# A two-layer hybrid decoder trunk: another opening, with positions and rotary tables taken early, one sum of squares, and more low parts made by DMA

## The chip, the cores and the metric

The kernel runs on one core of one Trainium2 chip. The metric is the device time of one execution in microseconds, as the median of several. The profile is one further execution with its instructions recorded; its times are counted from the span's start.

## The reference

The model has two layers over 512 tokens of width 1024. Layer 0 mixes tokens by retention (four heads, rotary positions on q and k), layer 1 by an mLSTM; each is followed by a convolutional feed-forward block of width 2816, and everything is normalised, shifted, scaled and gated by columns computed from a conditioning row c. Cut to what this change touches:

```python
c_act = silu(c)
for i in range(2):
    mod = c_act @ ada_w[i] + ada_b[i]
    sh_t, sc_t, gt_t, sh_f, sc_f, gt_f = split(mod, 6)
    h = rmsnorm(x, norm_tok_g[i]) * (1 + sc_t) + sh_t
    y = retention(h, positions, ...) if i == 0 else mlstm(h, ...)
    x = x + gt_t * y
    h = rmsnorm(x, norm_ffn_g[i]) * (1 + sc_f) + sh_f
    x = x + gt_f * conv_ffn(h, ...)
return rmsnorm(x, final_g)
# in retention:
proj = h @ w_in                     # q, k, v, g
ang = positions[..., None] * inv_freq
q, k = rope(q, cos(ang), sin(ang)), rope(k, cos(ang), sin(ang))
```

All is float32. The matrix products reach that precision with a split: a value is a high part in TensorE's single-pass float32 form plus a low part (the value less its high part), and a product is high by high, high by low and low by high.

## The kernel before, in words

Activations lie with features on the partitions: eight tiles x[0] to x[7] of 128 features by 512 tokens. Weights come in 128x1024 chunks. ScalarE casts a chunk to its high part (`high_part`), VectorE subtracts for the low part (`low_part`). The other way to a low part, `low_part_added`, has ScalarE write minus the high part and GpSimd issue an accumulating DMA that adds the raw chunk onto it.

**The planner.** Nothing is issued directly. Each call to an engine is recorded with the buffers that it reads and writes (`Plan.add`). A call gets an estimated cost: for TensorE by output width, with a factor for plain float32 operands; for DMAs by size. In `Plan.order` TensorE's costs are summed in program order, and a call of another engine is due 30 us after the TensorE time at which it was written, or earlier if a successor's due time, a cost and a latency ask for it. `Plan.run` then simulates the engines: each takes, among calls whose inputs are ready, the one with the earliest due time, and does not begin one that would hold up an urgent one. A call that opens a new buffer may not start over 30 us (`EARLY`) ahead of its due time. Calls made while `plan.pin` is set keep their written order on each engine. `after` adds an order to another call without data between them. The order that comes out is the order of the instructions on each engine; SP's DMA issues are planned in the same way.

**The opening** is `ret_start`. Loads of x, of c's row (`c_row`), an identity, columns of parameters (`vecs`), rows of the conditioning weights (`ada`) and weight chunks (`raw`, from `w_s0`) go through SP's queue. TensorE spreads c over the partitions (`pc`, plain float32 with one row), ScalarE puts it through silu into `c_ext`, and each modulation column is then one VectorE instruction over 1025 elements (`gemv`), the conditioning weights times `c_ext` with a running sum. Beside that ScalarE squares seven tiles of x and VectorE the eighth; VectorE adds them in three groups, whose sums TensorE contracts in three groups of one-column matmuls (`means`, tile `pms`). The root and reciprocal of the four columns are spread over partitions and tokens: VectorE writes four diagonal blocks (`diag`), and TensorE multiplies them by ones. `scaled` multiplies x by gain and root (`xr`), ScalarE adds the shift and casts (`hh`), VectorE makes the low part (`hl`). `busy(n)` puts dummy matmuls of 512 columns on TensorE: 3, 5, 2, 3 and 8 of them, in this order.

Then a loop over the eight tiles (`products`) multiplies h by the weights of head 0's v and g into eight PSUM banks, 24 matmuls a tile (`pst`, `pc`). Each step needs, from VectorE, two `gemv`, a gain, `scaled`, a weight's low part and h's low part.

After the loop come, in program order, the load of the positions (`posi`), the centering of v, the gate's silu, and `rope_tables`: a chain of 32 VectorE instructions over 128x512 (an argument reduction in `ra`, `rk`, `rn`, `rr`), then sine and cosine by ScalarE and GpSimd. Head 0's q and k follow as four chunks of 24 matmuls (`pp`), then `rope`, and for the later heads products folded in the manner of Strassen, whose operands (`t24`, `t3` and a rewritten half of h) VectorE makes in `sums_early`. The folded products (`p`) of head 1's q and k come next on TensorE.

**The end** is `End`, the last norm. The final contraction runs over the first 256 tokens of all eight tiles, then over the second 256. During the second half `later` is called after each tile: it makes the first half's root, and then calls `use_early`, which does nothing here; all output scalings and stores of the first half are written in `rest`, after the last contraction.

Of the kernel before, what the change touches and what calls it, by code (L numbers as in the profile page):

```python
# [16 lines left out]
P = 128  # L17
# [29 lines left out]

KINDS = {"s": NSLOTS, "w": WTILES, "a": 2, "ps": 8, "vm": 4, "dsh": 4}
HURRY = 1.5
SHARE = 1.4  # L50
EARLY = 30.0

# [4 lines left out]
VEC = {}  # L57
_at = 0
for _n, _w in (
    ("ntok", 2 * KT), ("nffn", 2 * KT), ("final", KT), ("rgn", 16), ("mgn", 16),  # L60
    ("mcw", 4 * 16), ("mcb", 16), ("fcw", 2 * 3 * 44), ("fcb", 2 * 44), ("bg", 2), ("inv", 1),
):
    VEC[_n] = _at
    _at += _w
# [72 lines left out]

class Call:
    __slots__ = ("eng", "name", "obj", "a", "k", "bufs", "preds", "succs", "occ", "lat", "dma", "due", "left", "ready",
                 "new", "fn", "pin", "after", "end", "shared")  # L140


class Plan:
    LAT = dict(PE=0.23, DVE=0.18, ACT=0.18, POOL=0.2, SP=0.1)

    def __init__(self):
        self.calls, self.pin = [], None

    def engine(self, eng, obj):
        plan = self  # L150
# [7 lines left out]
    def add(self, eng, obj, name, a, k):  # L158
        c = Call()
        c.eng, c.obj, c.name, c.a, c.k = eng, obj, name, a, k  # L160
        c.preds, c.succs, c.fn, c.pin, c.after = set(), [], None, self.pin, None
        n = len(self.calls)
        views = [(v, m == 0) for m, v in enumerate(a) if isinstance(v, View)]
        views += [(v, key == "accum_out") for key, v in k.items() if isinstance(v, View)]
        c.bufs = list({id(v.buf): v.buf for v, _ in views}.values())
        for v, w in views:
            self.note(n, c, v, w)
        c.dma = 0.0
        width = max([v.width for v, _ in views])
        if name == "dma_start":  # L170
            size = max((v.box[1] - v.box[0]) * v.width for v, _ in views) * 4e-6
            c.dma = size * (5.4 if "accum_op" in k else 2.45) + 0.05
            c.occ = 0.9 if eng == "POOL" else 0.4
        elif eng == "PE":
            o = a[0].width
            single = a[2].buf.args[2] == F32R and not any(s[0] == "bitcast" for s in a[2].steps)
            c.occ = max(o * 4.427e-4, 0.06) * (1 if single else 4)
        elif eng == "DVE":
            if name == "reciprocal":
                c.occ = 0.05 + 6.45e-3 * width  # L180
            elif name in ("tensor_scalar", "tensor_copy", "memset"):
                c.occ = 0.12 + 4.5e-4 * width
            else:
                c.occ = 0.09 + 1.06e-3 * width + (0.1 if "accum_out" in k else 0)
        elif eng == "ACT":
# [26 lines left out]
    def order(self):  # L212
# [26 lines left out]
            c.left = len(c.preds)  # L239

        for c in calls:
            c.due = pe_time + (0.0 if c.eng == "PE" else 30.0)
            pe_time += c.occ * (c.eng == "PE")
        for n in range(len(calls) - 1, -1, -1):
            c = calls[n]
# [12 lines left out]
    def run(self):  # L258
# [20 lines left out]
        def start_of(n, at):  # L279


            c = calls[n]
            t, need = max(at, c.ready), {}
            for b in c.bufs:
                if b.bufs and b.log is not None:
                    need[b.key] = need.get(b.key, 0) + 1
                    if bisect(makers[b.key], b.maker) > len(room[b.key]):
                        return None
            for key, k in need.items():
                if len(room[key]) < k:  # L290
# [89 lines left out]
def trunk(ctx: ExitStack, tc: tile.TileContext, xT, cb, pos, vec, ident, decay, zmask, ada, w_s0, w_in0, w_v0,  # L380
# [58 lines left out]
    posi = slot("posi", I32)  # L439

    def col(name, i):
        return vecs[:, VEC[name] + i : VEC[name] + i + 1]
# [749 lines left out]
    class End(Norm):  # L1192
# [348 lines left out]
    def ret_start():  # L1541
# [25 lines left out]
            wh[k] = high_part(raw[k])  # L1567

        def low(k):
            wl[k] = low_part(raw[k], wh[k])  # L1570

        def square(m):
            sq[m] = slot("sq")
            if m < 7:
# [4 lines left out]
        def add(a, b):  # L1579
            V.tensor_tensor(sq[b][:], sq[a][:], sq[b][:], op=ALU.add)  # L1580

        def means(m, last):

            for t in range(4):
                PE.matmul(ps[:, t : t + 1], sq[m][:, t * P : t * P + P], ones["d"][:, :1].bitcast(F32),
                          start=(m, t) == (3, 0), stop=last, skip_group_check=True)

        def products(k):
            hi, lo, st, sp = wh[k], wl[k], k == 0, k == KT - 1
# [7 lines left out]
        plan.pin = uid("pin")  # L1597
# [6 lines left out]
        S.dma_start(vecs[:, : VEC["nffn"]], vec[:, : VEC["nffn"]])  # L1604
        load_ada(KT)
        load_ada(0)
        load_raw(0)
# [5 lines left out]
        S.dma_start(vecs[:, VEC["nffn"] :], vec[:, VEC["nffn"] :])  # L1613
        silu_c = lambda i: A.activation(c_ext[:, i * T : i * T + T], pcs[i][:], AF.Silu)
        square(0)
        square(1)
        add(0, 1)
        silu_c(0)
        square(2)
        add(1, 2)  # L1620
        silu_c(1)
        square(3)
        add(2, 3)
        square(4)
        square(5)
        square(7)
        add(4, 5)
        square(6)
        add(6, 7)
        A.activation(rc[:, :1], eps_t[:], AF.Sqrt)  # L1630
        busy(5)
        means(3, False)
        busy(2)
        means(5, False)
        means(7, True)
# [3 lines left out]
        diag = slot("diag")  # L1639
        busy(3)  # L1640
        for t in range(4):
            cs = slice(t * P, t * P + P)
            V.tensor_scalar(diag[:, cs], eye[:, :P], rc[:, t : t + 1], None, op0=ALU.mult)
        for t in range(2):
            cs = slice(*HALVES[t])
            PE.matmul(ps[:, cs], ones["1"][:].bitcast(F32), diag[:, cs], start=True, stop=True,
                      skip_group_check=True)
        gain(0, 0, 0)
        gemv(0, 0, mod[0])
        high(0)  # L1650
        busy(8)
# [12 lines left out]
        for k in range(KT):  # L1664
            if k + 1 < KT:
                if k + 2 < KT:
# [7 lines left out]
                gemv(0, k + 1, mod[k + 1])  # L1674
# [3 lines left out]
        S.dma_start(posi[:], pos.broadcast_to([P, T]))  # L1678
# [4 lines left out]
        for _ in rope_tables():  # L1683
            pass
        return xrs

    def nothing(j):
# [11 lines left out]
    def ret_q(i, between=nothing):  # L1699
# [36 lines left out]
    def gates(ps):  # L1736
# [31 lines left out]
        S.dma_start(zm[:], zmask)  # L1768

    def conv_then(i, name, kt):  # L1770
        ch = (0 if name == "q" else 8) + i * 2 + kt
# [236 lines left out]
```

## Time and profile before

| | us |
|---|---|
| median of 3 runs | 1502.32 |
| lowest, highest run | 1498.59, 1504.9 |
| the profiled execution | 1497.61 |
| its span, first to last instruction | 1495.8 |
| TensorE busy in the span | 1468.1 |
| VectorE busy | 1264.9 |
| ScalarE busy | 1069.4 |
| GpSimd busy | 285.3 |

Nearly all instructions carry the same line number (that of the call in `Plan.issue`), so rows are told apart by tile names: output, an arrow, inputs, with buffer numbers left out. PE is TensorE's matmuls, PEld its weight loads, DVE VectorE, ACT ScalarE, POOL GpSimd, SP the sync engine. A row of the timeline has start, duration, engine, operation, tiles, shapes, a count, and in brackets how long the engine was idle before it and what ended that. Plain float32 products show as two rows for one matmul. Granted clock is the share of TensorE's clock that was allowed.

### The profile page before, as it was taken

To read this page: it belongs to the slowest core of one execution; us is meant where nothing else is said; L and a number is where in the kernel's file an instruction comes from. 1 tells how busy PE (TensorE), PEld (TensorE's weight loads), DVE (VectorE), ACT (ScalarE), POOL (GpSimd) and SP (SyncE) were. 2 spreads that over 40 slices of the span, in tenths; PEclk is the share of its full clock that TensorE was granted. 3 is DMA by queue.
4 is the path that set the end of the run, shared out by engine and by line. 5 is a ranking of instruction groups with operands and counts; after the bars stand their busy time and mean duration, and the time that the engine had idled before them with its cause. 6 is when DMAs were issued, how large, how long until landed. Compare 5 with 4: busy or idle time off the path is not lost.

```text
span 1495.8 us, 27226 instructions
## 1 busy us (share of the span) xinstructions
PE 1468.1 (98%) x10477; PEld 1373.1 (92%) x10477; DVE 1264.9 (85%) x2141; ACT 1069.4 (71%) x1601; POOL 285.3 (19%) x311
## 2 busy tenths in 40 slices
PE   9989999999999999999999999999999999999997
PEld 6889999998999999989999998999889899999997
DVE  6999979678988989888897999888889887877786
ACT  4558768877587766666569985889856876767652
POOL 0234223322111111111001231223231111111100
PEclk9999999999999999999999999999999999999998
DMA  9567989997788999999367995899796988877741
GB/s 376 162 162 178 293 193 242 226 284 203 180 225 213 251 246 265 254 243 267 110 195 155 238 230 148 184 230 211 234 261 176 220 224 197 206 191 168 196 130 57
DMA packets 92980, 315.00 MB, mean 211 GB/s; under 512 B 12193, under 2 KB 14625, under 8 KB 92850
## 3 DMA queue, kind: packets, MB, share of 16 engines
q0 software_dynamic: 31824, 115.88, 41.9%
q1 hardware_dynamic: 61026, 197.38, 37.8%
q8 instruction: 82, 1.34, 0.3%
q14 instruction: 48, 0.39, 0.1%
HBM read 195.23 MB, written 2.12 MB: 132 GB/s over the span
## 4 chain that ended last, share of the span: by engine, by line
PE 81%; DMA 7%; DVE 6%; issue 2%; ACT 2%; POOL 1%; DVEq 0%; POOLq 0%; SPq 0%; ACTq 0%
PE p L376 34%; PE po L376 23%; PE pv L376 7%; PE pp L376 5%; PE pf L376 4%; PE pav L376 3%; DMA wb<-w_up 2%; PE psc L376 2%; PE pst L376 2%; DMA wlo<-ws 2%; DMA ada<-ada 1%; DVE ada L376 1%; ACT whi L376 1%; DVE wlo L376 1%; DVE ws L376 1%
## 5 line engine op out<-in xcount | busy, mean ns | idle before, releaser
L376 PE MATMUL p<-hl,whi 128*128 128x256 f32 x992 | 275.5, 278 | 0.7 <-DVE hl L376 0.5
L376 PE MATMUL p<-hh,whi 128*128 128x256 f32 (+1 forms) x994 | 275.6, 278 | 0.0
L376 PE MATMUL p<-hh,wlo 128*128 128x256 f32 x992 | 273.9, 278 | 0.0
L376 ACT ACTIVATE wlo<-whi 128x1024 fp32r<-128x1024 f32 x221 | 233.2, 1060 | 54.9 <-PE po L376 25.3
L376 PEld LDWEIGHTS p<-hl,whi 128*128 128x128 f32 x992 | 187.1, 189 | 1.4 <-DVE hl L376 1.1
L376 PEld LDWEIGHTS p<-hh,whi 128*128 128x128 f32 x994 | 187.5, 189 | 0.4
L376 PEld LDWEIGHTS p<-hh,wlo 128*128 128x128 f32 x992 | 186.3, 188 | 0.1
L376 PE MATMUL p<-t24h,whi 128*128 128x256 f32 x744 | 166.7, 281 | 7.6 <-ACT fs L376 5.5
L376 PE MATMUL po<-ggl,whi 128*128 128x512 f32 (+1 forms) x448 | 153.2, 343 | 0.0
L376 PE MATMUL po<-ggh,wlo 128*128 128x512 f32 (+1 forms) x448 | 152.7, 343 | 0.0
L376 PE MATMUL po<-ggh,whi 128*128 128x512 f32 (+1 forms) x448 | 152.3, 343 | 0.0
L376 DVE SCALAR_TENSOR_TENSOR x<-po,mod,x 128x512 f32<-128x512 f32 (+1 forms) x184 | 112.6, 627 | 32.7 <-PE po L376 32.3
L376 PE MATMUL p<-t24l,whi 128*128 128x256 f32 x496 | 138.0, 278 | 0.0
L376 PEld LDWEIGHTS p<-t24h,whi 128*128 128x128 f32 x744 | 127.1, 189 | 11.4 <-ACT fs L376 6.9
L376 ACT CAST whi<-raw 128x1024 fp32r<-128x1024 f32 (+1 forms) x117 | 117.5, 1017 | 25.9 <-PE pf L376 4.6
L376 POOL DMA_DIRECT2D wlo<-wa x62 | 54.4, 878 | 411.4 <-ACT wlo L376 303.8
L376 DVE SCALAR_TENSOR_TENSOR ada<-ada,c_ext 128x1025 f32<-128x1025 f32 x96 | 120.1, 1252 | 7.0 <-DMA ada<-ada 7.0
L376 PE MATMUL po<-yh,whi 128*128 128x256 f32 (+1 forms) x354 | 116.0, 329 | 0.2 <-DVE x L376 0.2
L376 PE MATMUL po<-yl,whi 128*128 128x256 f32 (+1 forms) x352 | 115.9, 329 | 0.0
L376 PE MATMUL po<-yh,wlo 128*128 128x256 f32 (+1 forms) x352 | 115.2, 329 | 0.0
L376 DVE SCALAR_TENSOR_TENSOR cv<-p,vecs,cv 128x511 f32<-128x511 f32 (+1 forms) x144 | 106.2, 743 | 7.5 <-ACT cv L376 7.2
L376 ACT CAST whi<-ws 128x1024 fp32r<-128x1024 f32 x86 | 90.1, 1050 | 29.0 <-DVE ws L376 19.6
(285 smaller groups left out, 4428.3 us busy)
## 6 DMA issues: line engine op xcount, KB each, us to landing
ada<-ada SPq DMA_DIRECT2D x96, 512.5 KB, 7.2
wlo<-ws POOLq DMA_DIRECT2D x73, 512.0 KB, 7.4
wlo<-wa POOLq DMA_DIRECT2D x62, 512.0 KB, 6.9
wlo<-wt POOLq DMA_DIRECT2D x44, 512.0 KB, 6.9
wlo<-raw POOLq DMA_DIRECT2D x36, 512.0 KB, 8.4
wa<-w_up SPq DMA_DIRECT2D x36, 512.0 KB, 6.7
wb<-w_up SPq DMA_DIRECT2D x36, 512.0 KB, 6.8
raw<-w_o SPq DMA_DIRECT2D x32, 512.0 KB, 8.1
```

Source lines behind the costliest of these rows:

```text
L376: getattr(c.obj, c.name)(*[real(v) for v in c.a], **{key: real(v) for key, v in c.k.items()})
```

## The change

- **Loads.** c's row is the first load, x comes right behind it. The positions and the first columns of `vecs` are issued by ScalarE instead of SP. `inv` moves to the front of `vecs`, so that it comes with these columns. The weight chunk of tile 0 is loaded ahead of the second row of conditioning weights, and the remaining columns and the mask `zm` later.
- **Planner.** A call can carry `soon`, its offset from TensorE's time in place of the 30 us; it then also has no `EARLY` limit. Plain float32 matmuls are priced 8 instead of 4 times the single-pass ones, and the least price is 0.05 instead of 0.06.
- **Tables.** `rope_tables` is recorded at the beginning of `ret_start`, unpinned, with an offset of 200.
- **Squares.** ScalarE squares all tiles but x[3]; VectorE squares that and adds all eight in one chain; one group of `means` is left. The Sqrt dummy moves behind the square of x[4].
- **Roots.** No diagonals: each column of the reciprocal, repeated 128 times, is the weights of one product with the identity.
- **Dummies.** 3, 9, 1 and 1 instead of 3, 5, 2, 3 and 8.
- **Low parts.** Tiles 5, 6 and 7 of the loop, and the second chunks of head 0's q and k, use `low_part_added`.
- **End.** `use_early` scales and stores the first half's tiles during the second half, four at a time.

The diff, cut to its core:

```diff
+ROPE_DUE = 200.0
+BUSY = (9, 1, 1)
+LOWK = 5
+QLOW = (1, 3)
...
-            c.occ = max(o * 4.427e-4, 0.06) * (1 if single else 4)
+            c.occ = max(o * 4.427e-4, 0.05) * (1 if single else 8)
...
-            c.due = pe_time + (0.0 if c.eng == "PE" else 30.0)
+            c.due = pe_time + (0.0 if c.eng == "PE" else 30.0 if c.soon is None else c.soon)
...
-                t = max(t, c.due + lag - EARLY)
+                if c.soon is None:
+                    t = max(t, c.due + lag - EARLY)
...
+    c_load = len(plan.calls)
+    plan.soon = -8.0
     S.dma_start(c_row[:1, :D], cb)
     for m in range(KT):
-        S.dma_start(x[m][:], xT[m])
+        S.dma_start(x[m][:], xT[m]).after = c_load
+    plan.soon = -15.0
+    A.dma_start(vecs[:, : VEC["nffn"]], vec[:, : VEC["nffn"]])
+    A.dma_start(posi[:], pos.broadcast_to([P, T]))
+    plan.soon = None
...
         def use_early(self, k):
-            pass
+            if k in (2, 4):
+                self.use(0, 2 * k - 4, 2 * k)
         def rest(self):
-            item([], lambda w: self.use(0, 0, 4))
-            item([], lambda w: self.use(0, 4, 8))
...
-            wl[k] = low_part(raw[k], wh[k])
+            wl[k] = (low_part if k < LOWK else low_part_added)(raw[k], wh[k])
...
+        plan.soon = ROPE_DUE
+        for _ in rope_tables():
+            pass
+        plan.soon, plan.pin = None, uid("pin")
...
+        for m in range(KT):
+            square(m)
+            if m in (1, 2):
+                silu_c(m - 1)
+            if m == 4:
+                A.activation(rc[:, :1], eps_t[:], AF.Sqrt)
+            if m:
+                add(m - 1, m)
+        busy(BUSY[0])
+        means(KT - 1)
         gemv(0, KT, mod[KT])
+        gain(0, 0, 0)
+        high(0)
         A.activation(rc[:, :4], ps[:, :4], AF.Sqrt, bias=eps_t[:])
         V.reciprocal(rc[:, :4], rc[:, :4])
+        gemv(0, 0, mod[0])
+        busy(BUSY[1])
         for t in range(4):
+            PE.matmul(ps[:, t * P : t * P + P], rc[:, t : t + 1].broadcast_to([P, P]), eye[:, :P], start=True,
+                      stop=True, skip_group_check=True)
+        busy(BUSY[2])
...
+        first = len(plan.calls) - 3
...
+        S.dma_start(vecs[:, VEC["nffn"] :], vec[:, VEC["nffn"] :]).after = first
...
-                gemv(0, KT + k + 1, mod[KT + k + 1])
+                gemv(0, KT + k + 1, mod[KT + k + 1]).after = None if k else first
...
-                proj_item(w_in0[i * 8 + 2 * n + j], h0, then)
+                proj_item(w_in0[i * 8 + 2 * n + j], h0, then, 2 * n + j in QLOW)
```

More of the change, by code (lines that the diff above doesn't have):

```diff
@@ L59 @@
 for _n, _w in (
[L60 to L61 removed]
+    ("inv", 1), ("ntok", 2 * KT), ("nffn", 2 * KT), ("final", KT), ("rgn", 16), ("mgn", 16),
+    ("mcw", 4 * 16), ("mcb", 16), ("fcw", 2 * 3 * 44), ("fcb", 2 * 44), ("bg", 2),
 ):
@@ L139 @@
     __slots__ = ("eng", "name", "obj", "a", "k", "bufs", "preds", "succs", "occ", "lat", "dma", "due", "left", "ready",
-                 "new", "fn", "pin", "after", "end", "shared")
+                 "new", "fn", "pin", "after", "end", "shared", "soon")
 class Plan:
@@ L146, in __init__ @@
     def __init__(self):
-        self.calls, self.pin = [], None
+        self.calls, self.pin, self.soon = [], None, None
     def engine(self, eng, obj):
@@ L160, in add @@
         c.eng, c.obj, c.name, c.a, c.k = eng, obj, name, a, k
-        c.preds, c.succs, c.fn, c.pin, c.after = set(), [], None, self.pin, None
+        c.preds, c.succs, c.fn, c.pin, c.after, c.soon = set(), [], None, self.pin, None, self.soon
         n = len(self.calls)
@@ L439, in trunk @@
     posi = slot("posi", I32)
+    plan.soon = -15.0
+    A.dma_start(vecs[:, : VEC["nffn"]], vec[:, : VEC["nffn"]])
+    A.dma_start(posi[:], pos.broadcast_to([P, T]))
+    plan.soon = None
     def col(name, i):
@@ L1580, in add, with means @@
             V.tensor_tensor(sq[b][:], sq[a][:], sq[b][:], op=ALU.add)
-        def means(m, last):
+        def means(m):
             for t in range(4):
                 PE.matmul(ps[:, t : t + 1], sq[m][:, t * P : t * P + P], ones["d"][:, :1].bitcast(F32),
-                          start=(m, t) == (3, 0), stop=last, skip_group_check=True)
+                          start=t == 0, stop=True, skip_group_check=True)
         def products(k):
@@ L1603, in ret_start @@
         S.dma_start(eye[:, :P], ident)
-        S.dma_start(vecs[:, : VEC["nffn"]], vec[:, : VEC["nffn"]])
         load_ada(KT)
+        load_raw(0)
         load_ada(0)
-        load_raw(0)
         load_ada(KT + 1)
@@ L1612, in ret_start @@
         load_ada(2, aside("ada"))
-        S.dma_start(vecs[:, VEC["nffn"] :], vec[:, VEC["nffn"] :])
         silu_c = lambda i: A.activation(c_ext[:, i * T : i * T + T], pcs[i][:], AF.Silu)
[L1615 to L1635, printed above, removed]
+        for m in range(KT):
[8 more added lines that the diff above has]
+        means(KT - 1)
         gemv(0, KT, mod[KT])
+        gain(0, 0, 0)
+        high(0)
         A.activation(rc[:, :4], ps[:, :4], AF.Sqrt, bias=eps_t[:])
         V.reciprocal(rc[:, :4], rc[:, :4])
-        diag = slot("diag")
-        busy(3)
+        gemv(0, 0, mod[0])
+        busy(BUSY[1])
         for t in range(4):
[L1642 to L1651, printed above, removed]
+            PE.matmul(ps[:, t * P : t * P + P], rc[:, t : t + 1].broadcast_to([P, P]), eye[:, :P], start=True,
+                      stop=True, skip_group_check=True)
+        busy(BUSY[2])
         xr = xrs[0] = slot("xr")
@@ L1671, in ret_start @@
                 high(k + 1)
-                gemv(0, KT + k + 1, mod[KT + k + 1])
+                gemv(0, KT + k + 1, mod[KT + k + 1]).after = None if k else first
                 gain(0, 0, k + 1)
-                gemv(0, k + 1, mod[k + 1])
+                gemv(0, k + 1, mod[k + 1]).after = None if k else first
                 xrs[k + 1] = scaled(k + 1, slice(None), rs, 0, 0)
@@ L1682, in ret_start @@
             ret_gate(0)(pss[4 + j])
-        for _ in rope_tables():
-            pass
         return xrs
@@ L1767, in gates @@
                               allow_slow_non_contiguous=True)
-        S.dma_start(zm[:], zmask)
+        S.dma_start(zm[:], zmask).after = len(plan.calls) - 1
     def conv_then(i, name, kt):
```

4 lines of the change are left out of this document (1 added, 3 removed).

## The prediction

> **What bounds the kernel now.** I read the windows by stage first, then the opening engine by engine, then the chain of waits around 90 us, then the last 11 us. The windows (length; busy us and instructions of PE, PEld, DVE, ACT, POOL; granted clock; DMA share; GB/s):
>
> ```profile
> 0.00:21.70 21.70, 18.52 (x53) 13.23 (x54) 9.59 (x26) 10.31 (x18) 0.73 (x5) 1.00 0.94 349
> 21.70:65.40 43.70, 43.64 (x193) 35.79 (x192) 43.61 (x73) 19.00 (x24) 1.39 (x2) 1.00 0.80 287
> 65.40:87.40 22.00, 22.00 (x99) 18.22 (x98) 22.00 (x44) 15.27 (x27) 13.96 (x6) 1.00 0.40 92
> 90.40:99.60 9.20, 5.22 (x36) 4.22 (x34) 9.14 (x21) 7.32 (x15) 2.86 (x3) 0.93 0.26 86
> 99.60:105.00 5.40, 5.35 (x25) 5.35 (x26) 5.40 (x7) 3.43 (x5) 5.01 (x5) 0.50 0.82 244
> 1485.00:1495.80 10.80, 0.81 (x3) 0.30 (x2) 7.26 (x15) 0.89 (x2) 0.00 (x0) 0.62 0.55 194
> ```
>
> VectorE is full from 21.7 to 105 us (43.61 of 43.70, 22.00 of 22.00, 9.14 of 9.20) but works only 9.59 of the first 21.70. TensorE keeps pace until 90.4, then gets 36 matmuls done in 9.2 us. The chain that ended last has the same 24 matmuls on both sides of that hole:
>
> ```profile
> 87.53 2.84 PE p L376 x24
> ...
> 99.65 5.49 PE p L376 x24
> ```
>
> At 2.84 / 24 = 0.118 us each, the 36 need 4.3 us. From 90.37 to 99.65 is 9.28, so 5.0 are waiting. The clock is then granted at 0.50, and the next 24 cost 5.49 - 2.84 = 2.65 more. This hole costs 7.6 us. One small hole lies earlier, in the first pass over the eight input tiles: weight loads waiting 0.48 us for h.
>
> ```profile
> 32.83 0.30 PEld L376 LDWEIGHTS pst<-whi,hh 128*128 128x128 f32 x2 [0.48 <-ACT hh L376]
> ```
>
> **The opening.** TensorE's rows from the conditioning row to the first product that the output needs, and ScalarE's and SyncE's beside them:
>
> ```profile
> 4.83 3.77 PE L376 MATMUL pc<-c_row,ones 1*128 1x512 f32 x4 [1.86 <-DMA c_row<-cb]
> 8.53 2.50 PE L376 MATMUL pst<-warm,ones 128*128 128x512 f32 x5
> 10.83 1.70 PE L376 MATMUL pms<-ones_d,sq 128*128 128x1 f32 x8
> 12.39 1.20 PE L376 MATMUL pst<-warm,ones 128*128 128x512 f32 x2
> 13.39 3.41 PE L376 MATMUL pms<-ones_d,sq 128*128 128x1 f32 x16
> 16.66 1.63 PE L376 MATMUL pst<-warm,ones 128*128 128x512 f32 x3
> 18.09 1.94 PE L376 MATMUL pms<-diag,ones 128*128 128x256 f32 x4
> 19.52 2.35 PE L376 MATMUL pst<-warm,ones 128*128 128x512 f32 x8
> 21.72 1.08 PE L376 MATMUL pst<-whi,hh 128*128 128x512 f32 x4
> ```
> ```profile
> 8.64 0.60 ACT L376 ACTIVATE c_ext<-pc 128x512 f32<-128x512 f32 x1 [0.59 <-PE pc L376]
> 9.13 2.18 ACT L376 ACTIVATE sq<-x 128x512 f32<-128x512 f32 x4
> 11.33 1.28 ACT L376 ACT_TABLE_LOAD   x1
> 12.62 0.20 ACT L376 ACTIVATE rc<-eps_t 128x1 f32<-128x1 f32 x1
> 16.90 0.26 ACT L376 ACTIVATE rc<-pms,eps_t 128x4 f32<-128x4 f32 x1 [4.08 <-PE pms L376]
> ```
> ```profile
> 0.74 1.35 SPq L376 DMA_DIRECT2D x<-xT  x3
> 2.14 0.33 SPq L376 DMA_DIRECT2D c_row<-cb  x1
> ```
> ```profile
> 17.20 0.18 DVE L376 RECIPROCAL rc<-rc 128x4 f32<-128x4 f32 x1 [3.77 <-ACT rc L376]
> 17.41 0.88 DVE L376 TENSOR_SCALAR diag<-eye,rc 128x128 f32<-128x128 f32 x4
> ```
>
> *c first.* c's row is issued at 0.74 instead of 2.14, so the c products and the second silu of c move from 8.64 to about 7.24. x follows one issue later (0.33). *Squares.* ScalarE then does x4's square to 7.8, the Sqrt load (1.28) and its dummy (0.20) to 9.3, and three squares at 2.18 / 4 = 0.55 to 10.9; with slack for the positions' 256 KB ahead of x I take 11.4. VectorE's last addition ends near 12.2, where it ends today (10.99 + 1.29 = 12.28). So this part gains nothing by itself: the load that stood behind the squares now stands among them. *Means.* Sixteen one-column rows and two dummies follow that addition today, and the root starts at 16.90. Eight rows are left, half of 3.41 or 1.7, with about 0.5 of first load and drain: the root starts at 14.4, 2.5 earlier. *Spreading.* From the reciprocal's start to the end of the spread is 17.20 to 20.03, or 2.83. The diagonals (0.88) go; the four products with repeated columns have the same 512 columns in eight rows. A 256-column row takes 1.94 / 4 = 0.49, a one-column row 0.21 (the weight load), so eight cost 1.7 to 3.9. I take 2.4 from reciprocal to end, nearer the low end because 128 columns are half of 0.49, which gains 0.4; the high end loses 1.5. No trace here shows such a row. Together the first product moves from 21.5 to about 18.7, **2.8 us earlier**.
>
> On the ScalarE load: after it the next instruction starts at 12.62, 0.01 behind its end, so a moved load costs 1.28. The Trainium skill ("ScalarE: Activation LUTs", What ACT_TABLE_LOAD costs) adds about 1.38 of drain to every switch. By that page the squares, and with them the opening, would come 1.4 later and the whole change to 7.7 us; this trace speaks against it, and I give that outcome 0.02.
>
> *Clock.* 21 dummy matmuls become 14, and one instead of eight stands ahead of the first products. Five dummies cost 2.50 at 8.53, eight 2.35 at 19.52: the clock rises just before the products today. Afterwards TensorE idles for about a microsecond there and may start slow. The nearest row is 99.65, where a slow start cost 2.65; the bounds are 0 and the whole 5.4 us window at half speed, 2.7. I take 2.1. So the opening nets **0.7** (between -1.5 and 2.8). The Trainium skill ("TensorE: Matmul & The Clock Gate", Part 1) says the array runs at half rate until a free-running window of about 3.4 us has been busy. That speaks against cutting the dummies, and the 0.50 after the hole agrees; by it the loss could differ from run to run.
>
> Once TensorE starts slowly, VectorE has time in hand, so the 0.48 wait at 32.83 goes: **0.45**.
>
> **VectorE's relief.** Costs, as busy time by form to 105 us, and the transfer that replaces five subtractions:
>
> ```profile
> L376 DVE TENSOR_TENSOR wlo<-raw,whi 128x1024 fp32r<-128x1024 f32 x12 | 14.5, 1218 | 0.0
> L376 DVE SCALAR_TENSOR_TENSOR rr<-rk,rr 128x512 f32<-128x512 f32 x13 | 8.9, 684 | 0.0
> ...
> L376 DVE TENSOR_SCALAR rk<-rk 128x512 f32<-128x512 f32 x6 | 2.5, 419 | 0.0
> ```
> ```profile
> wlo<-raw POOLq DMA_DIRECT2D x36, 512.0 KB, 8.4
> ```
>
> The tables are 18 instructions of the 0.684 kind and 14 of the 0.419 kind: 12.3 + 5.9 = 18.2 us of VectorE, today all inside the full stretch. c's row took from 2.14 to 4.83; the positions, larger but first on a queue of their own, I give until 5. VectorE's free time until 18.7 takes a part: 21.70 - 9.59 = 12.1 are free today, some 4 of those lie before the positions land and 2.8 vanish with the earlier end, and the pieces between additions are short, so I take 4 us of tables (0 to 6). The rest still runs in the full stretch, in whatever order the planner gives it. Five low parts (three in the first pass, two for q and k) leave VectorE: 5 x 1.2 = 6.1. Relief is 4 + 6.1 = 10 us, against the 5.0 of waiting that it must cover plus about 1.2 by which TensorE arrives earlier. The five become ScalarE multiplications of about the same width, and ScalarE is busy 19.00 of 43.70 there; GpSimd issues five copies, idle but for 1.39. So the hole closes: **7.6**. Without the tables' share 6.1 would still just about cover it. What is late next is h's second halves, overwritten only after the q and k products stop reading them; TensorE needs them some 4 us after that, with four short casts and subtractions to do.
>
> **The tail.**
>
> ```profile
> 1484.88 2.46 DVE L376 SCALAR_TENSOR_TENSOR out<-x,vecs,rs 128x256 f32<-128x256 f32 x6
> 1487.25 1.75 DVE L376 RECIPROCAL rs<-rs 128x256 f32<-128x256 f32 x1
> 1489.04 3.25 DVE L376 SCALAR_TENSOR_TENSOR out<-x,vecs,rs 128x256 f32<-128x256 f32 x8
> ```
> ```profile
> 1486.21 0.47 ACT L376 ACTIVATE rs<-pms,eps_t 128x256 f32<-128x256 f32 x1 [0.79 <-PE pms L376]
> ```
>
> The second root is there at 1486.68, but six outputs of the first half hold VectorE until 1487.25. Moved among the last residuals, they leave the reciprocal free at about 1486.75: **0.5** (0 if the outputs then hold up a residual, 1 if the last writes also find emptier queues).
>
> The delayed mask, the moved vector columns and the second vector load run far ahead of their use: nothing. The sum is 0.7 + 0.45 + 7.6 + 0.5 = **9.2 us** off the profiled execution's 1497.6 (span 1495.8), which gives 1488.4. The median shown, 1502.32, lies 4.7 above that execution, and 1502.3 - 9.2 = **1493.1** is the forecast. Its own range is 6 to 12 us off, 1490 to 1496.
>
> **Rivals.** *The hole stays in part.* If the planner, whose table operations are now due late, runs them in the same crowded stretch and puts none ahead, or if ScalarE's extra work makes h late, some 3 us of waiting and slow clock remain where 7.6 were: 4.6 off, 1497.7. For it: VectorE has no free microsecond between 21.7 and 90. Against: the subtractions leave in any case. That the tables are not moved ahead at all is this case.
>
> *The rest is planned worse.* All due times and TensorE's prices for plain float32 shift, so every later order may change. The waits of TensorE's queue after 105 us are led by
>
> ```profile
> PE p L376 <- ACT fs L376: 6.0, 7, 1.8
> ```
>
> Two or three more of such waits (1.8 the longest) cost about 5: 4 off, 1498. The same lottery can give 3 back, and a first pass warm from the start gives 2.1 more: 12 to 15 off, 1489.
>
> *The low parts come late, and it gets slower.* The copies land 8.4 after issue; while the DMA engines are full (0.94 of the opening, 0.80 after it) that could double. A pass over one tile is 24 products of (1.08 - 0.39) / 3 = 0.23, or 5.5 us, so with raw tiles two passes ahead a copy may take 11 from negation to use. At 16.8 it is 5.8 late, TensorE waits and restarts at half clock (2.65): 8.5 in the first pass, and 8.5 again at the q and k weights, 17 against 9.2 gained: 7.8 slower, 1510. It decides from about 11 us of landing. Against: GpSimd has 1.39 us of other work in that whole stage, and the DMA share is down to 0.40 in the next.
>
> **Chances.** Forecast 0.55, better 0.08, hole in part 0.20, worse plan 0.08, late low parts 0.07, the table page 0.02. Half a percent, 7.5 us, is what a measurement of this kernel can tell from no change. Most of the forecast (0.47) and the better case lie beyond it: faster 0.56. Slower 0.08, the rest 0.36. The range runs from the better case to the worse plan, with the 3 us by which the runs shown stray on either side of their median: 1486 to 1501.
>
> **What would show it.** Right: the c products near 3.4 us, one group of eight mean rows, four repeated-column products, the first useful product near 18.7 with pitch 0.45 at first, the first third of the table operations before it, no granted clock of 0.50 near 100 us, and 36 matmuls there in 4 to 5 us; the reciprocal of the second half within 0.1 of its root. Wrong: TensorE waiting for wlo by DMA before 90 us, the hole at its place with VectorE still full, a first product after 20, or new waits of over 3 us behind 105.

## The result, and the profile after

| | before | after |
|---|---|---|
| median, us (6 runs each, same chip) | 1502.41 | 1490.94 |
| lowest, highest | 1498.55, 1504.9 | 1490.73, 1493.99 |
| ratio after/before, 95% interval | | 0.9931 [0.9913, 0.9949] |
| the profiled execution | 1497.61 | 1491.05 |
| its span | 1495.8 | 1489.3 |

The ratio, which is that of the means, says about 10 us faster (0.0069 x 1502). The forecast was 1493.1. The two profiled executions are only 6.5 us of span apart, because the one of before was quicker than all six of its timed runs: the places below add up to that 6.5, not to 10.

The windows by stage after the change, at four of the stretches shown for before (length; busy us and instructions of PE, PEld, DVE, ACT, POOL; granted clock; DMA share; GB/s):

```profile
0.00:21.70 21.70, 16.08 (x38) 10.24 (x39) 14.80 (x33) 11.41 (x19) 0.73 (x5) 0.82 0.87 338
21.70:65.40 43.70, 43.70 (x189) 36.00 (x189) 41.21 (x72) 23.35 (x28) 6.00 (x7) 0.97 1.03 325
90.40:99.60 9.20, 8.93 (x74) 8.62 (x73) 9.20 (x15) 6.49 (x10) 4.03 (x4) 1.00 0.95 306
99.60:105.00 5.40, 5.40 (x40) 5.17 (x39) 5.04 (x10) 1.99 (x4) 1.14 (x3) 1.00 1.05 240
```

Between 90.4 and 99.6 TensorE now starts 74 matmuls where it started 36, at a clock of 1.00, and behind that the clock stays at 1.00 instead of 0.50. That hole is closed. VectorE is still busy for all of the 9.20, but TensorE hardly waits for it any more. VectorE gets 5.21 us more done before 21.7 (14.80 against 9.59) and has 2.49 us free in the long pass (41.21 of 43.70). ScalarE's 23.35 there against 19.00, and GpSimd's 7 instructions against 2, are the low parts by DMA.

The opening on TensorE (start, duration, engine, operation, tiles, shapes, count, and in brackets the idle time ahead and what ended it):

```profile
2.89 3.78 PE L381 MATMUL pc<-c_row,ones 1*128 1x512 f32 x4
6.60 4.06 PE L381 MATMUL pst<-warm,ones 128*128 128x512 f32 x9
14.27 1.87 PE L381 MATMUL pms<-ones_d,sq 128*128 128x1 f32 x8 [3.62 <-DVE sq L381]
16.00 0.77 PE L381 MATMUL pst<-warm,ones 128*128 128x512 f32 x1
16.77 2.08 PE L381 MATMUL pms<-eye,rc 128*128 128x128 f32 x8
18.50 0.77 PE L381 MATMUL pst<-warm,ones 128*128 128x512 f32 x1
19.96 2.07 PE L381 MATMUL pst<-whi,hh 128*128 128x512 f32 x4 [0.69 <-ACT hh L381]
```

The first product starts at 19.96, against 21.72 before and a forecast of 18.7. Then four matmuls take 2.07 where they took 1.08: TensorE starts at half its clock. The eight rows that multiply repeated columns by the identity, which the trace of before could not show, take 2.08, near the low end of the 1.7 to 3.9 given for them. Of dummies only the single ones at 16.00 and 18.50 are left here.

ScalarE and VectorE beside it:

```profile
5.86 0.63 ACT L381 ACTIVATE sq<-x 128x512 f32<-128x512 f32 x1 [2.73 <-DMA x<-xT]
...
9.66 1.28 ACT L381 ACT_TABLE_LOAD   x1
10.95 0.20 ACT L381 ACTIVATE rc<-eps_t 128x1 f32<-128x1 f32 x1
11.06 1.65 ACT L381 ACTIVATE sq<-x 128x512 f32<-128x512 f32 x3
...
16.24 0.26 ACT L381 ACTIVATE rc<-pms,eps_t 128x4 f32<-128x4 f32 x1 [1.60 <-PE pms L381]
```
```profile
6.30 0.43 DVE L381 CAST ra<-posi 128x512 f32<-128x512 int32 x1 [4.89 <-DMA posi<-pos]
...
10.35 3.87 DVE L381 TENSOR_TENSOR sq<-sq,sq 128x512 f32<-128x512 f32 x5
...
16.54 0.18 DVE L381 RECIPROCAL rc<-rc 128x4 f32<-128x4 f32 x1 [0.32 <-ACT rc L381]
```

The first square starts at 5.86 because x was not there, the last ends at 12.71 (11.06 + 1.65), the last addition at 14.22 (10.35 + 3.87), the means start at 14.27, and the root starts at 16.24. VectorE's first table step waits 4.89 for the positions.

In the tail the second half's reciprocal now follows its root at once, 1480.72 behind 1480.21 + 0.47 = 1480.68; before, it waited from 1486.68 to 1487.25. Three outputs of the first half stand at 1477.09, ahead of the last residual, and only the second half's eight are left behind the reciprocal.

```profile
1480.21 0.47 ACT L381 ACTIVATE rs<-pms,eps_t 128x256 f32<-128x256 f32 x1 [0.79 <-PE pms L381]
```
```profile
1477.09 1.27 DVE L381 SCALAR_TENSOR_TENSOR out<-x,vecs,rs 128x256 f32<-128x256 f32 x3
...
1480.72 1.75 DVE L381 RECIPROCAL rs<-rs 128x256 f32<-128x256 f32 x1 [1.75 <-ACT rs L381]
1482.51 3.25 DVE L381 SCALAR_TENSOR_TENSOR out<-x,vecs,rs 128x256 f32<-128x256 f32 x8
```

From the last `po` matmul to the end it is 11.06 us, against 11.59 before.

Landmarks from the trace, and the time that TensorE lost by stretch. A loss is the sum, over the matmuls of a stretch, of the distance from one start to the next beyond 0.4435 ns per column (the pitch of a 512-column row at full speed, 0.227 us); it counts waiting and slow clock alike.

| us | before | before, copy | after | after, copy |
|---|---|---|---|---|
| first product | 21.72 | 22.73 | 19.96 | 19.53 |
| first q and k product (`pp`) | 65.61 | 66.27 | 65.49 | 65.68 |
| lost, 88 to 112 | 8.3 | 7.7 | 1.3 | 0.7 |
| lost, 112 to 160 | 1.1 | 1.1 | 3.4 | 3.3 |
| lost, 160 to 500 | 9.1 | 10.8 | 8.2 | 8.1 |
| lost, 500 to 700 | 5.7 | 6.1 | 3.7 | 7.1 |
| lost, 700 to 1300 | 18.5 | 17.9 | 20.3 | 19.2 |

The copies are the unchanged kernels, profiled beside the experiments. The 6.5 us of the first pair are 0.1 at the q and k products, 7.0 at the hole and 0.5 in the tail, less 1.1 that is given back in between. The last rows warn: two profiles of the same kernel differ by 3.4 us between 500 and 700 alone, so a few us in the later stages can't be given to any edit from one profile. Most of these 3.4 lie at one place. In the copy's chain of waits a load of feed-forward weights (`wb`) lands at 657.0, what depends on it comes late, TensorE waits 2.1 for `fs`, and the clock is 0.50 from 663.1 to 666.6. From 655 to 675 TensorE starts 119 matmuls at a granted clock of 0.91; in the first profile it is 154 at 1.00.

### The profile page after: what moved, and what is told of

It reads as the page before. It is cut to its first block, busy times and chain, and to the rows that moved or that the text cites. A ratio compares the mean times of both kernels' runs of the same rounds, so it can differ in the third digit from the quotient of the medians.

```text
span 1489.3 us, 27204 instructions
## 1 busy us (share of the span) xinstructions
PE 1464.2 (98%) x10458; PEld 1369.3 (92%) x10458; DVE 1261.0 (85%) x2134; ACT 1074.2 (72%) x1606; POOL 286.9 (19%) x316
## 4 chain that ended last, share of the span: by engine, by line
PE 78%; DVE 9%; DMA 7%; issue 3%; ACT 2%; POOL 1%; SPq 0%; DVEq 0%; POOLq 0%; ACTq 0%
PE p L381 33%; PE po L381 25%; PE pv L381 6%; PE pf L381 4%; PE pav L381 4%; PE pp L381 3%; PE psc L381 2%; DMA wlo<-ws 2%; DMA wlo<-wt 1%; DMA wb<-w_up 1%; DVE ada L381 1%; DVE wlo L381 1%; DMA raw<-w_in 1%; DMA ada<-ada 1%; DVE ws L381 1%
## 5 line engine op out<-in xcount | busy, mean ns | idle before, releaser
L381 ACT ACTIVATE wlo<-whi 128x1024 fp32r<-128x1024 f32 x226 | 238.6, 1060 | 55.0 <-PE po L381 25.2
L381 POOL DMA_DIRECT2D wlo<-ws x73 | 63.3, 867 | 247.6 <-ACT wlo L381 126.6
```

The costliest lines, as they stand in the source:

```text
L381: getattr(c.obj, c.name)(*[real(v) for v in c.a], **{key: real(v) for key, v in c.k.items()})
```

## The experiments

All ratios are against the kernel before, run on the same chip. None of these kernels leaves out a part of the computation.

| kernel | median, us | ratio, 95% interval | first product | `pp` | lost, 88 to 112 |
|---|---|---|---|---|---|
| before, unchanged copy | 1500.24 | 1.0007 [0.9993, 1.0021] | 22.73 | 66.27 | 7.7 |
| tables_late | 1489.48 | 0.9934 [0.9912, 0.9956] | 19.83 | 65.02 | 2.2 |
| no_dma_lows | 1491.46 | 0.9943 [0.9921, 0.9965] | 19.49 | 65.70 | 4.1 |
| neither | 1494.19 | 0.9970 [0.9951, 0.9989] | 19.76 | 65.25 | 8.1 |
| before_dma_lows | 1493.74 | 0.9951 [0.9933, 0.9969] | 22.62 | 66.16 | 1.8 |
| before_new_prices | 1496.05 | 0.9972 [0.9956, 0.9987] | 22.68 | 66.24 | 7.0 |
| old_prices | 1491.35 | 0.9953 [0.9936, 0.9969] | 19.84 | 65.79 | 1.5 |
| dummies_8 | 1492.05 | 0.9948 [0.9929, 0.9968] | 22.20 | 65.84 | 1.3 |
| pos_after_x | 1487.81 | 0.9927 [0.9903, 0.9952] | 19.36 | 65.13 | 0.6 |
| cols_after_x | 1492.52 (one run) | | 20.34 | 64.01 | 1.8 |
| pos_after_x_dummies | 1490.72 | 0.9932 [0.9913, 0.9951] | 19.11 | 63.25 | 0.8 |
| after, unchanged copy | 1492.52 | 0.9945 [0.9926, 0.9963] | 19.53 | 65.68 | 0.7 |

The theory: the gain is VectorE's relief closing the hole at 90 to 100 us, and either part of the relief does most of it. The rivals: the tables taken early are what matters, the low parts are, or the gain lies elsewhere (the opening, the tail, other orders from new prices).

**Does the spread of the runs come from the clock?** The unchanged kernel before:

> The kernel before once more, for the span and the granted clock of each of its runs. Theory A (the clock): the hole near 90 us lets the clock fall for a stretch that depends on where the clock's window lies, and the first pass starts warm or not, so runs differ by up to 6 us and the longer runs have the lower granted clock. Rival B (transfers): runs differ as much but at the same clock. Ratio to the kernel before 0.998 to 1.002.

It ran from 1497.98 to 1502.96, and its chip's other runs of the kernel before from 1495.46 to 1506.34. The granted clock of these runs was 0.993 to 0.997. On the whole the longer runs have the lower clock: of the 77 runs of the kernel before beside the experiments, the 23 at 0.994 or less average 1501.9 us, and the 54 at 0.995 or more 1498.7. So Theory A holds in part, but only in part: 1506.34 had 0.994, 1495.46 had 0.995, 1498.62 had 0.997. Whether the clock lengthens a run, or a late transfer does and the clock falls behind it, as in the copy at 657 us, is not shown.

**The hole: tables late, no low parts by DMA, neither.** The tables are recorded where before has them:

```diff
-        plan.soon = ROPE_DUE
-        for _ in rope_tables():
-            pass
         plan.soon, plan.pin = None, uid("pin")
...
             ret_gate(0)(pss[4 + j])
+        for _ in rope_tables():
+            pass
```

> The changed kernel with the table chain recorded where it stood before (after the first pass), all else as changed. Theory 1 (VectorE's relief adds up): the five low parts alone take 6 us off VectorE, against some 5 us of waiting, so the hole near 90 us stays mostly closed: 0 to 2 us slower than the changed kernel, some 1491 to 1493. Rival 2 (the tables' place decides): the hole is back with the clock at 0.50 behind it, 5 to 8 us slower, 1496 to 1499.

The five low parts go back to VectorE:

```diff
-LOWK = 5
-QLOW = (1, 3)
+LOWK = 8
+QLOW = ()
```

> The changed kernel with all low parts of the opening and of head 0's q and k on VectorE again. Theory 1: the eight table instructions that now run before 19 us are 4 us of relief, a little less than the waiting to be covered, so 1 to 3 us of waiting come back near 90 us, perhaps with the clock: 1 to 5 us slower than the changed kernel, 1492 to 1496. Rival 2 (the tables' place decides): no difference, 1490 to 1492. Rival 3 (the low parts decide): the whole hole is back, 6 to 8 us slower.

Both at once (`neither`):

> The changed kernel with both the table chain at its old place and all low parts on VectorE: what is left of the change is the opening's order, the prices and the end. Theory 1 (either relief is enough, none is not): the hole near 90 us is back with 6 to 8 us lost between 88 and 112 us, as before the change, and the time is 5 to 8 us above the changed kernel, ratio to the kernel before 0.996 to 1.001. Rival 5 (the hole was closed by the new order as such, by the early positions or the prices): no loss of more than 3 us there, ratio 0.992 to 0.995.

The low parts alone, put into the kernel before:

```diff
-            wl[k] = low_part(raw[k], wh[k])
+            wl[k] = (low_part if k < 5 else low_part_added)(raw[k], wh[k])
...
-                proj_item(w_in0[i * 8 + 2 * n + j], h0, then)
+                proj_item(w_in0[i * 8 + 2 * n + j], h0, then, 2 * n + j in (1, 3))
```

> The kernel before with nothing but the five low parts of the change made by DMA. Theory 1 (either relief is enough): the loss between 88 and 112 us falls from 8 us to 2 or 3, with no granted clock of 0.50 near 100 us, and the time falls by 4 to 6 us, ratio 0.996 to 0.997 or a little under. Rival 10 (the low parts work only together with the new opening): the hole stays, ratio 0.999 to 1.001.

The window 90.4 to 99.6 (and behind it for `neither`) in the order tables_late, no_dma_lows, neither, before_dma_lows, columns as above:

```profile
90.40:99.60 9.20, 9.20 (x79) 9.16 (x78) 8.97 (x14) 6.95 (x12) 7.81 (x6) 1.00 0.54 190
```
```profile
90.40:99.60 9.20, 7.78 (x65) 7.54 (x64) 9.04 (x17) 6.81 (x11) 5.81 (x5) 1.00 0.59 195
```
```profile
90.40:99.60 9.20, 5.20 (x34) 4.17 (x33) 9.20 (x21) 7.33 (x14) 3.09 (x3) 0.89 0.25 86
99.60:105.00 5.40, 5.40 (x28) 5.36 (x28) 5.40 (x7) 3.40 (x6) 4.66 (x5) 0.56 0.93 255
```
```profile
90.40:99.60 9.20, 9.20 (x79) 9.16 (x78) 8.02 (x13) 6.77 (x11) 7.38 (x6) 1.00 1.01 325
```

79, 65, 34 and 79 matmuls. With one relief left the hole is closed (tables late) or half closed (low parts back); with both gone it is as before, 34 matmuls with VectorE at 9.20 of 9.20, and a clock of 0.56 behind it. The low parts alone close it in the kernel before: 8.3 or 7.7 lost become 1.8, and the ratio is 0.9951. So the low parts are the stronger half, as 6.1 against 4 us of VectorE made likely. This is also the one experiment in which closing the hole shows in the whole time by itself: five low parts, and about 7 us. The whole times of the first two can't be told from those of the changed kernel: their intervals overlap. `neither`, with the hole open, is by the ratios 4 to 6 us slower than the changed kernel and its copy, where 5 to 8 were expected; its interval overlaps that of the copy.

**The opening.** The first question is what made x late. Columns and positions behind x on SP's queue (`pos_after_x`), and the columns alone (`cols_after_x`, positions as in the change):

```diff
-    plan.soon = -15.0
-    A.dma_start(vecs[:, : VEC["nffn"]], vec[:, : VEC["nffn"]])
-    A.dma_start(posi[:], pos.broadcast_to([P, T]))
+    plan.soon = -6.0
+    S.dma_start(vecs[:, : VEC["nffn"]], vec[:, : VEC["nffn"]]).after = c_load + KT
+    S.dma_start(posi[:], pos.broadcast_to([P, T])).after = c_load + KT
```

> The changed kernel with the positions and the first columns on SyncE's queue right behind the eight tiles of x instead of on ScalarE's queue beside them. Theory 6 (the small transfers beside x hold x up): the first square starts near 4.1 us instead of 5.9, the last addition ends near 12.3 instead of 14.2, the first product comes 1.5 to 2 us earlier, and q and k's first product (65.5 us) 1 to 2 us earlier; the time falls by as much, 0.1 per cent, at the edge of what can be measured. Rival 7 (x is held up by going behind c's row and by its own queue): the first square stays after 5 us and nothing moves. Fewer table instructions run ahead of 19 us; by theory 1 the low parts still cover that.

> As the one before, but only the columns (128 pieces of 68 bytes) go behind x; the positions (128 pieces of 2 KB) stay on ScalarE's queue. If the small pieces hold x up, the first square starts near 4.3 us; if the positions do, it stays at 5.5 or later.

The tile view of x, from issue to landing, for before, its copy, after and pos_after_x:

```profile
DMA to landing us min/median/max: 2.9/3.2/3.8
```
```profile
DMA to landing us min/median/max: 2.6/4.0/4.4
```
```profile
DMA to landing us min/median/max: 4.5/5.4/5.9
```
```profile
DMA to landing us min/median/max: 2.6/4.0/5.6
```

ScalarE's squares in pos_after_x and then cols_after_x:

```profile
3.73 1.26 ACT L381 ACTIVATE sq<-x 128x512 f32<-128x512 f32 x2 [1.50 <-DMA x<-xT]
...
6.96 0.63 ACT L381 ACTIVATE sq<-x 128x512 f32<-128x512 f32 x1 [1.35 <-DMA x<-xT]
```
```profile
5.93 1.27 ACT L381 ACTIVATE sq<-x 128x512 f32<-128x512 f32 x2 [3.29 <-DMA x<-xT]
```

With both loads behind x the first square starts at 3.73 instead of 5.86 (4.47 to 5.48 in the six other profiles that keep the two loads where the change puts them); with only the columns moved it stays at 5.93. x lands as in the copy of before. It is the load of the positions beside x that makes x late, by 1.4 (5.4 against 4.0). The other profiles agree: the median is 5.2 to 5.5 in the eight with the positions beside x, and 3.2 to 4.3 in the six without. But the third square then waits for x until 6.96, and the last ends at 12.00 instead of 12.71. The first product comes at 19.36: 0.6 before that of after, but only 0.1 before the earliest of its other profiles (19.49), and not the 1.5 to 2 expected. VectorE's additions there show the second limit:

```profile
8.95 1.49 DVE L381 TENSOR_TENSOR sq<-sq,sq 128x512 f32<-128x512 f32 x2
10.91 0.43 DVE L381 CAST ra<-posi 128x512 f32<-128x512 int32 x1 [0.47 <-DMA posi<-pos]
11.25 2.28 DVE L381 TENSOR_TENSOR sq<-sq,sq 128x512 f32<-128x512 f32 x3
```

Three additions, each on the result of the one ahead, take 2.28, a pitch of (2.28 - 0.69) / 2 = 0.80, and a table step that waited for the positions stands between them.

The second question is what the start at half clock costs: eight dummies ahead of the first product instead of one (`dummies_8`), and then, on top of pos_after_x, 14 and three (`pos_after_x_dummies`).

```diff
-BUSY = (9, 1, 1)
+BUSY = (9, 1, 8)
```

> The changed kernel with eight dummy matmuls instead of one ahead of the first products. Theory 8 (a cold start costs 2 us): eight dummies at half clock are 3.4 us and hold TensorE from 18.5 until 21.9, past the 20.0 at which h is ready, so the first product comes 1.5 to 2 us later, but the clock rises before or just behind it and the 24 products of the first tile take 5.5 to 7 us instead of 7.5; q and k's first product stays within 1 us of 65.5. Rival 9 (the first pass is held by transfers or VectorE anyway, so that its start does not matter): the same 65.5 whatever the clock does, with waits inside the pass instead.

```diff
-BUSY = (9, 1, 1)
+BUSY = (14, 1, 3)
```

> The changed kernel with the positions and first columns behind x, and with 14, 1 and 3 dummy matmuls instead of 9, 1 and 1, placed where TensorE stands idle anyway. Theory 8 (the cold start costs 2 us): the clock rises up to one window earlier, the first pass takes 43.6 to 45 us instead of 45.6, and q and k's first product is 0.3 to 2 us before that of the changed kernel; 1 to 4 us below the changed kernel. Rival 9: no difference to the run without the additional dummies.

The window 19.3 to 24 of after, dummies_8 and pos_after_x_dummies:

```profile
19.30:24.00 4.70, 4.04 (x10) 3.17 (x11) 4.67 (x9) 3.37 (x5) 0.00 (x0) 0.50 1.03 418
```
```profile
19.30:24.00 4.70, 4.70 (x16) 3.74 (x15) 4.70 (x9) 3.38 (x5) 0.00 (x0) 1.00 1.02 416
```
```profile
19.30:24.00 4.70, 4.70 (x21) 3.90 (x22) 4.59 (x9) 2.26 (x4) 0.00 (x0) 1.00 1.02 418
```

The first line has a clock of 0.50. The 1.00 of the second counts only from 22.41, where this trace has its first record of the clock; ahead of that the eight dummies take 3.76, or 0.47 each, the pitch at half clock. So there the clock comes up just behind the first product, which starts at 22.20. In the third it is up from 19.29. From first product to `pp` it is 65.49 - 19.96 = 45.5 us in after and 65.84 - 22.20 = 43.6 in dummies_8: the slow start costs 1.9. But eight dummies delay the first product by 2.2, which also gives the other engines 2.2 more to prepare, and `pp` is no earlier. The cleaner pair is pos_after_x and pos_after_x_dummies, with first products 0.25 apart: 65.13 - 19.36 = 45.8 against 63.25 - 19.11 = 44.1, so 1.6, and `pp` is 1.9 earlier. The whole time does not show it: 0.9927 without and 0.9932 with these dummies, where the changed kernel has 0.9931 and, in its copy, 0.9945.

The start is not slow in every execution, nor is a quick one always worth something. With the dummies of the change the clock came up at 19.04 in cols_after_x (`pp` at 64.01) and at 19.00 in `neither`, ahead of the first product. `neither` still has `pp` at 65.25: without the relief VectorE is busy 39.13 of the 40 us from 24 to 64 there (37.53 in after), and TensorE waits 1.1 for h inside the pass.

**The prices.** They are two numbers in the planner, and touch no computation. New prices alone in the kernel before, and old prices in the changed kernel:

```diff
-            c.occ = max(o * 4.427e-4, 0.06) * (1 if single else 4)
+            c.occ = max(o * 4.427e-4, 0.05) * (1 if single else 8)
```

> The kernel before with nothing but the planner's new prices for plain float32 matmuls. Theory 1: the hole near 90 us stays (7 to 8 us lost between 88 and 112 us) and the ratio is 0.998 to 1.002, its distance from 1 being what a mere shift of due times is worth. Rival 4 (the prices make the new order): the hole closes or waits of 3 us or more go or come elsewhere.

> The changed kernel with the planner's old prices for plain float32 matmuls (factor 4, least price 0.06). Theory 1: the prices shift all due times together, so the opening and the stretch to 105 us keep their order within an instruction or two and the time stays within 1.5 us of the changed kernel. Rival 4 (the prices make the new order): waits near 90 us or behind 105 us change by 3 us or more either way.

The window of the hole in before_new_prices:

```profile
90.40:99.60 9.20, 5.98 (x44) 5.38 (x44) 8.51 (x19) 7.34 (x15) 3.57 (x3) 0.90 0.38 134
```

The hole stands (44 matmuls, 7.0 lost), and yet the kernel is 0.9972 [0.9956, 0.9987] of before, some 4 us faster. Theory 1 had 0.998 to 1.002, and the rival a closed hole or long waits elsewhere; neither came. So in the kernel before the prices have a gain of their own. `neither`, which has these prices, the opening and the end but no relief, is no better than that (0.9970): in the whole time the opening and the end add nothing that can be measured. Taking the prices out of the changed kernel gives 0.9953, which is slower but overlaps the changed kernel, so their share there is not shown. Its profile has one bad stretch, 11.1 us lost between 160 and 325 against 5.6: TensorE waits 2.9 for `p` and 2.1 for `fs`, and the clock is 0.50 from 321.7 to 325.1. Where the 4 us of before_new_prices lie can't be read from its profile, since single profiles differ by as much in the later stages.

**The changed kernel once more**, beside the last runs:

> The changed kernel once more, on the chip of the other three. Ratio 0.991 to 0.995, as before; the loss between 88 and 112 us is 1 to 2 us, and q and k's first product is at 65 to 66 us.

0.9945 [0.9926, 0.9963]: about 8 us, with the hole closed again (0.7 lost) and `pp` at 65.68.

## Why the prediction was right, and where it was not

**The hole: right.** Predicted 7.6, measured 8.3 - 1.3 = 7.0 in the stretch itself. The sum of reliefs held too: 3.8 us of tables ahead of the first product (predicted 4; eight of the 32 steps, not the third expected), and five low parts of 1.2. "Without the tables' share 6.1 would still just about cover it" is tables_late, with 2.2 lost. The low parts did not come late: in the trace of after no matmul before 105 us waits for one, and over the whole run such loads land as fast as before.

```profile
wlo<-raw POOLq DMA_DIRECT2D x41, 512.0 KB, 8.4
```

The rival that made it slower needed 11 us; the median is 8.4 again, and those issued before 105 us land after 4.6 to 10.0.

**The opening: the step that failed.** "Together the first product moves from 21.5 to about 18.7" was the step. (The row of before has the first product at 21.72, not 21.5.) It came at 19.96, and in the other profiles with the changed opening as recorded between 19.49 and 19.84. The parts behind the additions were right: the root 2.0 after the last addition (predicted 14.4 - 12.2 = 2.2), and 2.31 from the reciprocal's start to the end of the spread (16.54 to 18.85; predicted 2.4). What was mis-sized is "VectorE's last addition ends near 12.2". It ends at 14.22. I had given x one issue of delay (0.33) and some slack for the positions; the squares end at 12.71 instead of 11.4. About 0.7 of these 1.3 is the positions beside x, since pos_after_x ends them at 12.00; what the rest is stays open. The other 0.7 is the chain of additions: before made its last two on different sums and they took 1.29, a pitch of 0.60; the change makes one chain, and five take 3.87, a pitch of 0.80. That the dependence causes the longer pitch was not tried by itself; the pairs differ in that, and every dependent group here has 0.80.

The other end of that step moves too. The eight dummies ahead of the first product, 2.35 in the row of before that I read, took longer in its copy, in before_dma_lows and in before_new_prices:

```profile
19.61 3.27 PE L376 MATMUL pst<-warm,ones 128*128 128x512 f32 x8
```
```profile
19.55 3.23 PE L376 MATMUL pst<-warm,ones 128*128 128x512 f32 x8
```
```profile
18.95 3.89 PE L376 MATMUL pst<-warm,ones 128*128 128x512 f32 x8
```

Their first products start at 22.73, 22.62 and 22.68, and `pp` at 66.27, 66.16 and 66.24. The profiled execution of before was a quick one: the clock came up at 19.84 in it, and at 21.90, 21.76 and 22.61 in these. Against them the first product is some 2.9 earlier, which equals the forecast's 2.8 by accident: about 1 of it is dummies at half clock that no longer stand there.

The c products were early (2.89; predicted near 3.4). On ScalarE's load of the Sqrt table, after's row agrees with before's: 9.66 + 1.28 = 10.94, and the next instruction starts at 10.95. The extra 1.38 of drain that the Trainium skill ("ScalarE: Activation LUTs", What ACT_TABLE_LOAD costs) states does not show. (By that page the whole change would come to 9.2 - 1.4 = 7.8, not the 7.7 written.)

**The cold start: right.** Predicted 2.1, measured 1.9 by dummies_8 and 1.6 by the cleaner pair. The wait of 0.48 at 32.83 is gone. At `pp` the forecast was 0.7 + 0.45 = 1.15; measured are 0.12 between the two profiled executions (65.61 to 65.49), and 0.6 from the copies (66.27 to 65.68). The opening gave half of its term or less.

**The tail: right.** Predicted 0.5, measured 11.59 - 11.06 = 0.53. It was not run by itself.

**The prices: not counted.** They stood in the text as a lottery that could cost 5 or give 3 back, outside the sum. In the kernel before they give some 4 us by themselves, with some 2 us of uncertainty; how much of that is left in the changed kernel is not shown. That the forecast of 9.2 came out so near the measured 8 to 10 is in part luck. The opening was short and this term was missing. The profiles, prices included, account for 6.5 us of span (6.3 in the copies), and where the rest of the 8 to 10 lies is open. And the base, the median of 1502.3, was a high one: beside the experiments the medians of the kernel before were 1498.9, 1499.7 and 1500.0. No wait over 3 us appeared behind 105; the longest there, for the low part of a folded weight, is 2.2 against 1.9 before.

```profile
PE p L381 <- ACT fs L381: 3.6, 6, 1.0
PE p L381 <- DMA wlo<-ws: 2.2, 1, 2.2
```

The waits for `fs`, which I feared would grow, fell from 6.0 to 3.6. In exchange 112 to 160 loses 2.3 us more than before, in both profiles of the changed kernel. That belongs to one order of the plan and not to the closed hole as such: tables_late, no_dma_lows, old_prices and pos_after_x lose 1.1 to 1.3 there.

## What to carry to other kernels

An engine that looks hidden over the whole run can still be the bound in one stretch: find the stretch where it is full and the next engine waits, and count relief against the waiting there; the relief beyond that cover brought nothing that could be measured here. A load moved to another engine's queue can still slow the loads beside it, so a "free" early load may be paid for by one that is needed first, as the positions were by x. Where a planner orders the work, run its changed prices alone before crediting the edits that came with them, and expect that a gain of 2 us in the opening is not visible against runs that spread over 5 to 10.

## What the runs showed of the hardware

The clock can be earned and lost within the opening. In after it comes up as the nine dummies end at 10.36: they took 4.06 / 9 = 0.45 each, the pitch at half clock. (The clock's first record is at 10.36; ahead of it the column shows 1.00 for want of one.) The window view shows it go (columns as above):

```profile
6.60:10.36 3.76, 3.76 (x10) 2.81 (x9) 3.62 (x9) 3.34 (x6) 0.00 (x0) 1.00 1.06 406
10.36:13.77 3.41, 0.30 (x2) 0.00 (x0) 3.00 (x5) 2.52 (x6) 0.00 (x0) 1.00 1.03 421
13.77:24.00 10.23, 9.04 (x28) 7.16 (x29) 9.56 (x19) 4.50 (x7) 0.00 (x0) 0.50 1.02 417
```

In the 3.41 us from 10.36 TensorE is busy for 0.30, and then the clock is 0.50 until 24.0 though it is busy for 9.04 of the next 10.23, with one-column means and 128-column rows among them. The Trainium skill ("TensorE: Matmul & The Clock Gate", Part 1) gives 3413 ns for the window that decides, and says that it runs freely, without regard to the kernel's start; the 3.41 us here agree, and so do the rises between 19.84 and 22.61 in four profiles of one opening or nearly one. What share of a window must be busy is not settled by these runs.

A load of 256 KB that spreads one 2 KB row of positions over 128 partitions, issued beside the eight 256 KB loads of x, took the median landing of x to 5.4 us (5.2 to 5.5 in eight profiles), from 3.2 to 4.3 in the six profiles without it.
